# Feature-major operands turned by 32x32 block transposes on VectorE, and the first two column blocks of two projections multiplied by turns

## The chip, the cores and the metric

The kernel runs on one core of one Trainium2 chip. The metric is the time of one execution on the device in microseconds (us). Before the change the median of three runs is 1024.64 us (1023.89 to 1025.12).

## The reference

One layer of a decoder trunk, 256 tokens by 2048 features, everything in float32. A normalised input is multiplied by one wide matrix; three branches (block-sparse attention A, windowed attention B, a gated linear recurrence C) are built from its columns, each is gated and projected back to 2048 features, weighted by a sigmoid gate, and the three are summed. What the change touches comes after that:

```python
merged = jnp.einsum('bsnd,bsnd->bsd', gates, y_d)       # sum of the three gated branches
x = x + merged @ w_out                                  # 2048 x 2048
x = x + jax.nn.sigmoid(rmsnorm(x, ple_norm_g) @ w_pg) * (p_i @ w_pp)   # w_pg: 2048 x 2048
# output: rmsnorm(x, final_norm_g)
```

## The kernel before

**Tiling.** TensorE (PE) multiplies with the contracted features on the 128 partitions. An operand in "feature-major" form has features on partitions and the 256 tokens along the row; a result comes out "token-major", two halves (h = 0, 1) of 128 tokens on partitions and 512 columns of the output (one column block) along the row. A product over 2048 features takes 16 steps (k) of 128 features. Full precision is reached with three passes: both operands are split into a high part (a rounded copy, made by ScalarE, ACT) and a low part (the rest, made by VectorE, DVE), and `mm3` issues high x high, high x low, low x high. So a column block of `project` is 16 steps x 2 halves x 3 = 96 matmuls of 128x512.

**Weights.** They stream from memory in tiles of 128x1024, that is, two steps k of a column block; `fetch` loads one on SP's queue, `split` casts it on ACT (L112, `wh`) and subtracts on DVE (L113, `wl`). There are four buffers for raw tiles (`wraw`) and four for split ones (`wsp`): tile number i+4 can be cast only after PE has done with tile i.

**The two stages around the change.** `merge` (L618) runs for the three branches; for the last of them (`bi == 2`), after each of the four column blocks n, DVE multiplies the branch by its gate (L631), adds it into `merged` (L632), and `turn` (L604) brings these 512 features of `merged` to feature-major form, as operand `m` (`mT`) of the product with `w_out`. That loop (L654) computes column block after column block; for each, DVE adds the residual (L657, which also frees the PSUM tile), ACT sums squares (L660), and `turn` makes the operand `x2` of the product with `w_pg`, multiplied by the norm's gain (`split_scaled`, L191). The last loop (L678) multiplies by `w_pg`, applies the sigmoid and writes the output.

**`turn` before.** For 512 features it issues 8 transposes of 128x128 on PE (L610, a matmul against an identity) into two PSUM tiles `tp`, four into each. Then the halves are split from PSUM: without a gain an ACT copy (L180) and a DVE subtract (L181) of 128x512 for each of the two tiles; with a gain four ACT scalings (L193) and four DVE operations (L194) of 128x256. It is called eight times, four times for `m`, four times for `x2`.

**PSUM.** Products write to one of two tiles (`matrix_psum`, two banks for each), `tp` comes from four other banks.

**Order of the work.** Each engine runs its queue in order. A planner writes the queues at build time: among the instructions that are ready in its own timing model it takes the one that stands first in the program, except that a weight tile's cast and subtract are moved up by `LEAD` = 100 places (`high_priority`, L106). A tile of a column block takes 13 places in the program, its load and its 12 matmuls. DVE's queue holds, besides the `wl` subtractions, everything named DVE above.

Of the kernel before, what the change touches and what calls it, by code (L numbers as in the profile page):

```python
# [17 lines left out]
P = 128  # L18
D = 2048
SEQ = 256  # L20
NH = SEQ // P
BW = D // 2
KD = D // P
KB = BW // P
CW = 512
WT = 1024
# [11 lines left out]
NEG = -1e30  # L38
SLOT = 2112
WPAD = 64  # L40
WOFF = 32
RV = 384
B_ORDER = [g0 * 4 + s * 4 + i for g0 in (0, 2) for i in range(4) for s in range(2)]
# [3 lines left out]
def trunk(ctx: ExitStack, tc: tile.TileContext, x, xt, p, table, onehot, maskv, w_in, sinks, conv, w_ri, vec, fin, w_br,  # L47
          w_out, w_pg, w_pgt, w_pp, out):
    nc = tc.nc
# [9 lines left out]
    def block(name, dtype=F32):  # L59
        return blk.tile([P, SLOT], dtype, tag="blk", name=name)  # L60
# [4 lines left out]
    def cols(k, n=1):  # L65
        return slice(k * SEQ, (k + n) * SEQ)

    def aux(name):
        return ps_x.tile([P, CW], F32, tag="aux", name=name)

    def temp(name):
        return small.tile([P, 4, SEQ], F32, tag="tmp", name=name, bufs=4)

    ident = const.tile([P, P], F32, name="ident")
# [18 lines left out]
    def fetch(src, i, name, pieces=1):  # L93
        r = wraw.tile([P, WT], F32, tag="raw", name=f"r_{name}")
        n = WT // pieces
        for j in range(pieces):
            loads.append(nc.sync.dma_start(r[:, j * n : (j + 1) * n], src[i][:, j * n : (j + 1) * n]).ins)
        raws[name] = r, pieces

    def split(name, off):  # L100
        r, pieces = raws.pop(name)
        hi = wsp.tile([P, WT + WPAD], F32R, tag="whi", name=f"wh_{name}")[:, off : off + WT]
        lo = wsp.tile([P, WT + WPAD], F32R, tag="wlo", name=f"wl_{name}")[:, off : off + WT]
        n = WT // pieces
# [11 lines left out]
    def mm3(ps, a, b, first, last):  # L116
        (ah, al), (bh, bl) = a, b
        nc.tensor.matmul(ps, ah, bh, start=first, stop=False)  # L118
        nc.tensor.matmul(ps, ah, bl, start=False, stop=False)  # L119
        nc.tensor.matmul(ps, al, bh, start=False, stop=last)  # L120

    def weights_of(src, row, name, sub, off=0):
        held = {}

        def get(k):
            s = k // sub
            if s not in held:
                key = f"{name}_{s}"
                if key not in raws:
                    fetch(src, row + s, key)  # L130
                held[s] = split(key, off)
            return held[s], k % sub

        return get

    def matrix_psum(name):
        return ps_mm.tile([P, NH, CW], F32, tag="mm", name=f"ps_{name}")

    def project(act, src, row, name, cw=CW, weights=None, half=None, hooks={}):
        nk = len(act)  # L140
        if half is None:
            ps = matrix_psum(name).rearrange("p h c -> p (h c)")
        else:
            ps = aux(f"ps_{name}_{half}")
        get = weights or weights_of(src, row, name, WT // cw)
        for k in range(nk):
            w, kk = get(k)
            if k in hooks:
                with tc.issue_after(casts[-1]):
                    hooks[k]()  # L150
            c = slice(kk * cw, (kk + 1) * cw)
            for h in range(NH) if half is None else [half]:
                o = h * cw if half is None else 0
                q = slice(h * P, (h + 1) * P)
                mm3(ps[:, o : o + cw], [t[:, q] for t in act[k]], [t[:, c] for t in w],
                    k == 0 and o % CW == 0, k == nk - 1 and (half is not None or (o + cw) % CW == 0))
        return ps if half is not None else ps[:, : NH * cw].rearrange("p (h c) -> p h c", h=NH)

    def project_turned(row, name):
        ps = matrix_psum(name)  # L160
        get = weights_of(w_in, row, name, WT // SEQ, WOFF)
        for k in range(KD):
# [11 lines left out]
    def act_of(*units):  # L174
        return [tuple(t[:, cols(k)] for t in u) for u in units for k in range(KB)]

    def split_act(u, k, n, src):
        uh, ul = u
        o = cols(k, n)
        ins = nc.scalar.copy(uh[:, o], src).ins  # L180
        nc.vector.tensor_tensor(ul[:, o], src, uh[:, o].bitcast(F32), op=ALU.subtract)  # L181
        return ins
# [8 lines left out]
    def split_scaled(pair, src, scale):  # L191
        hi, lo = pair
        ins = nc.scalar.activation(hi, src, AF.Copy, scale=scale).ins  # L193
        nc.vector.scalar_tensor_tensor(lo, src, scale, hi.bitcast(F32), op0=ALU.mult, op1=ALU.subtract)  # L194
        return ins
# [70 lines left out]
    for b in range(4):  # L266
        t = block(f"h{b}", F32R)
# [28 lines left out]
    for n in range(4):  # L296
        ps = project(act_of(pT)[:2], w_pp, n, f"pp{n}")
        o = token_major(temp(f"pp{n}"))
# [303 lines left out]
    mT = []  # L602

    def turn(u, n, src, name, gain=None):  # L604
        for j in range(0, 4, 2):
            pt = aux(f"tp_{name}{n}{j}")
            for i in range(2):
                for h in range(NH):
                    c = n % 2 * CW + (j + i) * P
                    nc.tensor.transpose(pt[:, i * SEQ + h * P : i * SEQ + (h + 1) * P], src[:, h, c : c + P], ident)  # L610
            k = n % 2 * 4 + j
            if gain is None:
                split_act(u, k, 2, pt)
            else:
                for i in range(2):
                    split_scaled([t[:, cols(k + i)] for t in u], pt[:, cols(i)], gain[:, 4 * n + j + i : 4 * n + j + i + 1])

    def merge(z, bi, br):  # L618
        if bi == 0:
# [32 lines left out]
    x2T = [unit("x20"), unit("x21")]  # L652
    sq2 = const.tile([P, NH, 4], F32, name="sq2")
    for n in range(4):  # L654
        ps = project(act_of(*mT), w_out, n * KD * CW // WT, f"out{n}")
        sl = xr[n // 2][:, :, half_cols(n)]
        nc.vector.tensor_tensor(sl, ps, sl, op=ALU.add)  # L657
        junk = token_major(temp(f"jy{n}"))
        for h in range(NH):
            nc.scalar.activation(junk[:, h, :], sl[:, h, :], AF.Square, accum_out=sq2[:, h, n : n + 1])  # L660
        turn(x2T[n // 2], n, xr[n // 2], "x2", ple_g)
# [16 lines left out]
    for n in range(5):  # L678
        cw = CW if n < 3 else HW
        at = n * CW if n < 3 else 3 * CW + (n - 3) * HW  # L680
        b, lc = at // BW, slice(at % BW, at % BW + cw)
        if n < 3:
            parts = project(act_of(*x2T), w_pg, n * KD * CW // WT, f"pg{n}")
        elif n == 3:
            parts = project(act_of(*x2T), w_pgt, 0, f"pg{n}", cw=HW)
        y = token_major(temp(f"y{n}"))
        junk = token_major(temp(f"jz{n}"))
        ws = weights_of(w_pgt, KD * HW // WT, f"pg{n}", WT // HW)
        for h in range(NH):
            if n == 4:  # L690
                ps = project(act_of(*x2T), None, 0, f"pg{n}", cw=HW, weights=ws, half=h)[:, :HW]
            else:
                ps = parts[:, h, :]
            yh, xh = y[:, h, :cw], xr[b][:, h, lc]
            nc.scalar.activation(yh, ps, AF.Sigmoid, scale=rs2[:, h : h + 1])
            nc.vector.tensor_tensor(yh, yh, pps[b][:, h, lc], op=ALU.mult)
            nc.vector.tensor_tensor(xh, xh, yh, op=ALU.add)
            if n < 4:
                nc.scalar.activation(junk[:, h, :cw], xh, AF.Square, accum_out=sq3[:, h, n : n + 1])
                nc.gpsimd.tensor_tensor(xh, xh, fg[:, at : at + cw], op=ALU.mult)  # L700
                continue
            t, r = tot3[:, h : h + 1], rs3[:, h : h + 1]
            nc.vector.tensor_tensor_reduce(junk[:, h, :cw], xh, xh, op0=ALU.mult, op1=ALU.add, scale=1.0,
                                           scalar=0.0, accum_out=t)
            nc.vector.tensor_scalar(t, t, 1.0 / D, part[:, h : h + 1], op0=ALU.mult, op1=ALU.add)
            nc.gpsimd.tensor_tensor(r, t, half_c[:, :1], op=ALU.pow)
            nc.vector.tensor_tensor(xh, xh, fg[:, at : at + cw], op=ALU.mult)
            for eng, c0, c1 in ((nc.sync, 0, BW), (nc.scalar, BW + CW, D), (nc.sync, BW, BW + CW)):
                sl = xr[c0 // BW][:, h, c0 % BW : c0 % BW + c1 - c0]
                if eng is nc.sync:  # L710
                    nc.vector.tensor_scalar_mul(sl, sl, r)
                else:
                    nc.scalar.activation(sl, sl, AF.Copy, scale=r)
                eng.dma_start(out[h * P : (h + 1) * P, c0:c1], sl)
        if n == 3:
            nc.vector.reduce_sum(part, sq3, axis=AX.X)
            nc.vector.tensor_scalar(part, part, 1.0 / D, EPS, op0=ALU.mult, op1=ALU.add)
# [80 lines left out]
```

## Time and profile before

| | before |
|---|---|
| median of three runs | 1024.64 us |
| profiled execution | 1025.27 us |
| its span, first to last instruction | 1023.5 us |
| PE busy | 1011.1 us (99% of the span), 5216 matmuls |
| DVE busy | 643.5 us (63%) |
| ACT busy | 540.9 us (53%) |
| mean granted TensorE clock | 0.997 of 2.4 GHz |

An engine's busy time is the time in which at least one of its instructions runs. Matmuls overlap one another (each is recorded with some 0.39 us, and the next begins 0.23 us later), so what a matmul costs is read from the distance of starts, not from its duration. PEld is the load of a matmul's stationary operand, which runs beside the matmuls. The profiled execution is 1.8 us longer than its span.

### The profile page before, as it was taken

To read this page: it belongs to the slowest core of one execution; us is meant where nothing else is said; L and a number is where in the kernel's file an instruction comes from. 1 tells how busy PE (TensorE), PEld (TensorE's weight loads), DVE (VectorE), ACT (ScalarE), POOL (GpSimd) and SP (SyncE) were. 2 spreads that over 40 slices of the span, in tenths; PEclk is the share of its full clock that TensorE was granted. 3 is DMA by queue.
4 is the path that set the end of the run, shared out by engine and by line. 5 is a ranking of instruction groups with operands and counts; after the bars stand their busy time and mean duration, and the time that the engine had idled before them with its cause. 6 is when DMAs were issued, how large, how long until landed. Compare 5 with 4: busy or idle time off the path is not lost.

```text
span 1023.5 us, 13704 instructions
## 1 busy us (share of the span) xinstructions
PE 1011.1 (99%) x5216; PEld 860.2 (84%) x5216; DVE 643.5 (63%) x923; ACT 540.9 (53%) x762; POOL 30.2 (3%) x22
## 2 busy tenths in 40 slices
PE   8999999999999999999999999999999999999996
PEld 7788888888888888888988888888888888888886
DVE  5866956668866755456556677667545555555564
ACT  6744445558567654444445656655444444444552
POOL 0000000000000000000000001000000000000122
PEclk9999999999999999999999999999999999999998
DMA  9866655554646555555554555465555665576552
GB/s 330 291 220 214 202 194 176 181 174 156 206 165 209 178 174 201 188 191 196 185 187 158 190 188 184 144 199 171 183 187 185 223 236 180 187 271 224 201 184 84
DMA packets 58201, 199.52 MB, mean 195 GB/s; under 512 B 6600, under 2 KB 10008, under 8 KB 57624
## 3 DMA queue, kind: packets, MB, share of 16 engines
q1 hardware_dynamic: 51840, 186.41, 54.8%
q10 hardware_dynamic: 6296, 12.24, 3.4%
q8 instruction: 41, 0.67, 0.3%
q14 instruction: 24, 0.20, 0.1%
HBM read 194.40 MB, written 4.23 MB: 194 GB/s over the span
## 4 chain that ended last, share of the span: by engine, by line
PE 96%; DMA 2%; issue 1%; ACT 0%; DVE 0%; SPq 0%; POOLq 0%; POOL 0%; ACTq 0%; DVEq 0%
PE ps_in L166 21%; PE ps_in L168 11%; PE ps_in L119 10%; PE ps_in L118 10%; PE ps_in L120 10%; PE ps_out L120 3%; PE ps_out L118 3%; PE ps_out L119 3%; PE ps_pg L118 3%; PE ps_pg L119 3%; PE ps_pg L120 3%; PE ps_bra L120 1%; PE ps_bra L119 1%; PE ps_bra L118 1%; PE ps_brc L119 1%; PE ps_brc L118 1%
## 5 line engine op out<-in xcount | busy, mean ns | idle before, releaser
L113 DVE TENSOR_TENSOR wl_in<-r_in,wh_in 128x1024 fp32r<-128x1024 f32 x232 | 288.7, 1251 | 183.3 <-ACT wh_in L112 181.3
L112 ACT CAST wh_in<-r_in 128x1024 fp32r<-128x1024 f32 x232 | 242.9, 1050 | 268.1 <-PE ps_in L166 142.8
L166 PE MATMUL ps_in<-h,wh_in 128*128 128x512 f32 x928 | 289.9, 393 | 0.0
L168 PEld LDWEIGHTS ps_in<-h,wl_in 128*128 128x128 f32 x928 | 173.6, 188 | 39.4
L119 PE MATMUL ps_in<-wl_in,h 128*128 128x512 f32 (+1 forms) x480 | 184.7, 385 | 0.7 <-DVE wl_in L113 0.7
L168 PE MATMUL ps_in<-h,wl_in 128*128 128x256 f32 x928 | 185.0, 280 | 0.0
L118 PE MATMUL ps_in<-wh_in,h 128*128 128x512 f32 (+1 forms) x480 | 184.4, 385 | 0.0
L120 PE MATMUL ps_in<-wh_in,h 128*128 128x512 f32 (+1 forms) x480 | 183.8, 383 | 0.0
L166 PEld LDWEIGHTS ps_in<-h,wh_in 128*128 128x128 f32 x928 | 142.3, 188 | 0.2
L119 PEld LDWEIGHTS ps_in<-wl_in,h 128*128 128x128 f32 x480 | 90.3, 188 | 18.7 <-DVE wl_in L113 1.1
L118 PEld LDWEIGHTS ps_in<-wh_in,h 128*128 128x128 f32 x480 | 90.3, 188 | 17.6
L120 PEld LDWEIGHTS ps_in<-wh_in,h 128*128 128x128 f32 x480 | 90.3, 188 | 17.2
L113 DVE TENSOR_TENSOR wl_pg<-r_pg,wh_pg 128x1024 fp32r<-128x1024 f32 x32 | 39.8, 1243 | 38.3 <-ACT wh_pg L112 38.3
L113 DVE TENSOR_TENSOR wl_out<-r_out,wh_out 128x1024 fp32r<-128x1024 f32 x32 | 39.2, 1224 | 37.4 <-ACT wh_out L112 37.4
L112 ACT CAST wh_out<-r_out 128x1024 fp32r<-128x1024 f32 x32 | 33.7, 1054 | 42.5 <-PE ps_out L120 36.5
L112 ACT CAST wh_pg<-r_pg 128x1024 fp32r<-128x1024 f32 x32 | 33.7, 1052 | 41.9 <-PE ps_pg L120 33.5
L120 PE MATMUL ps_pg<-wh_pg,x_lo 128*128 128x512 f32 (+1 forms) x160 | 55.4, 347 | 0.0
L119 PE MATMUL ps_pg<-wl_pg,x_hi 128*128 128x512 f32 (+1 forms) x160 | 55.3, 347 | 0.0
L118 PE MATMUL ps_pg<-wh_pg,x_hi 128*128 128x512 f32 (+1 forms) x160 | 55.3, 347 | 0.0
L119 PE MATMUL ps_out<-wl_out,m_hi 128*128 128x512 f32 x128 | 50.1, 391 | 0.0
L118 PE MATMUL ps_out<-wh_out,m_hi 128*128 128x512 f32 x128 | 49.9, 390 | 0.0
L120 PE MATMUL ps_out<-wh_out,m_lo 128*128 128x512 f32 x128 | 49.8, 389 | 0.0
(273 smaller groups left out, 1271.4 us busy)
## 6 DMA issues: line engine op xcount, KB each, us to landing
r_in<-w_in_dram SPq DMA_DIRECT2D x232, 512.0 KB, 3.5
r_out<-w_out_dram SPq DMA_DIRECT2D x32, 512.0 KB, 3.4
r_pg<-w_pg_dram SPq DMA_DIRECT2D x24, 512.0 KB, 3.5
r_brc<-w_br_dram SPq DMA_DIRECT2D x16, 512.0 KB, 3.5
r_bra<-w_br_dram SPq DMA_DIRECT2D x16, 512.0 KB, 3.8
r_brb<-w_br_dram SPq DMA_DIRECT2D x16, 512.0 KB, 4.0
r_pg<-w_pgt_dram SPq DMA_DIRECT2D x8, 512.0 KB, 4.2
x<-xt_dram SPq DMA_DIRECT2D x4, 512.0 KB, 7.2
```

The source lines that it names most:

```text
L112: casts.append(nc.scalar.copy(hi[:, c], r[:, c]).ins)
L113: nc.vector.tensor_tensor(lo[:, c], r[:, c], hi[:, c].bitcast(F32), op=ALU.subtract)
L118: nc.tensor.matmul(ps, ah, bh, start=first, stop=False)
L119: nc.tensor.matmul(ps, ah, bl, start=False, stop=False)
L120: nc.tensor.matmul(ps, al, bh, start=False, stop=last)
L166: nc.tensor.matmul(ps[:, j, :], wh[:, cs[j]], h_both[k], start=k == 0, stop=False)
L168: nc.tensor.matmul(ps[:, j, SEQ:], wl[:, cs[j]], h_act[k][0], start=False, stop=k == KD - 1)
```

## The change

`turn` no longer uses PE. It takes a temporary in SBUF and fills it with 16 VectorE transposes: each reads 32 partitions (one quarter of the tokens of a half, index q) and writes 32 partitions (one quarter of the features, index f), 256 elements in each row, as eight blocks of 32x32 (two halves x four groups of 128 features). The source quarter q changes with every instruction, the destination quarter f with every fourth. The splits then read this temporary: without a gain one ACT copy and one DVE subtract of 128x1024 in place of two of each of 128x512, with a gain four and four as before, from SBUF in place of PSUM.

The second part reorders matmuls. `project_two` allocates two PSUM tiles and multiplies column blocks 0 and 1 by turns: steps k = 0 to 11 of block 0, the same of block 1, then k = 12 to 15 of block 0, then of block 1. It is used for `w_out` and `w_pg`; blocks 2 and 3 are as before. What follows block 0 (residual, squares, `turn`; or sigmoid and output) and what follows block 1 now both come after `project_two` in the program.

```diff
+    def project_two(act, src, names, late):
+        pss = [matrix_psum(n) for n in names]
+        gets = [weights_of(src, i * KD * CW // WT, n, WT // CW) for i, n in enumerate(names)]
+        for ks in (range(late), range(late, KD)):
+            for ps, get in zip(pss, gets):
+                for k in ks:
+                    w, kk = get(k)
+                    c = slice(kk * CW, (kk + 1) * CW)
+                    for h in range(NH):
+                        q = slice(h * P, (h + 1) * P)
+                        mm3(ps[:, h], [t[:, q] for t in act[k]], [t[:, c] for t in w], k == 0, k == KD - 1)
+        return pss
...
     def turn(u, n, src, name, gain=None):
-        for j in range(0, 4, 2):
-            pt = aux(f"tp_{name}{n}{j}")
-            for i in range(2):
-                for h in range(NH):
-                    c = n % 2 * CW + (j + i) * P
-                    nc.tensor.transpose(pt[:, i * SEQ + h * P : i * SEQ + (h + 1) * P], src[:, h, c : c + P], ident)
-            k = n % 2 * 4 + j
-            if gain is None:
-                split_act(u, k, 2, pt)
-            else:
-                for i in range(2):
-                    split_scaled([t[:, cols(k + i)] for t in u], pt[:, cols(i)], gain[:, 4 * n + j + i : 4 * n + j + i + 1])
+        t = temp(f"tn_{name}{n}")
+        c0 = n % 2 * CW
+        quad = [slice(i * QD, (i + 1) * QD) for i in range(P // QD)]
+        for f in quad:
+            for q in quad:
+                d = t[f].rearrange("p j (h q) -> p h j q", h=NH)[:, :, :, q]
+                s = src[q, :, c0 : c0 + CW].rearrange("p h (j f) -> p h j f", j=4)[:, :, :, f]
+                nc.vector.transpose(d, s)
+        k = n % 2 * 4
+        if gain is None:
+            split_act(u, k, 4, t.rearrange("p j q -> p (j q)"))
+        else:
+            for i in range(4):
+                split_scaled([o[:, cols(k + i)] for o in u], t[:, i, :], gain[:, 4 * n + i : 4 * n + i + 1])
...
     for n in range(4):
-        ps = project(act_of(*mT), w_out, n * KD * CW // WT, f"out{n}")
+        if n == 0:
+            pss = project_two(act_of(*mT), w_out, ["out0", "out1"], KD - 4)
+        ps = pss[n] if n < 2 else project(act_of(*mT), w_out, n * KD * CW // WT, f"out{n}")
...
-        if n < 3:
+        if n == 0:
+            two = project_two(act_of(*x2T), w_pg, ["pg0", "pg1"], KD - 4)
+        if n < 2:
+            parts = two[n]
+        elif n == 2:
             parts = project(act_of(*x2T), w_pg, n * KD * CW // WT, f"pg{n}")
```

## Rows read from the trace of the kernel before

**Rows 1.** The page: span, busy time of each engine (share), and its chain.

```profile
span 1023.5 us, 13704 instructions
PE 1011.1 (99%) x5216; PEld 860.2 (84%) x5216; DVE 643.5 (63%) x923; ACT 540.9 (53%) x762; POOL 30.2 (3%) x22
PE 96%; DMA 2%; issue 1%; ACT 0%; DVE 0%; SPq 0%; POOLq 0%; POOL 0%; ACTq 0%; DVEq 0%
```

**Rows 2.** All waits of PE: waiter, whom for, us in total, times, longest.

```profile
PE ps_pp L118 <- ACT wh_pp L112: 1.4, 1, 1.4
PE busy L262 <- DVE sp L353: 1.1, 1, 1.1
PE ps_in L119 <- DVE wl_in L113: 0.7, 1, 0.7
PE ps_pp L119 <- DVE wl_pp L113: 0.2, 1, 0.2
```

**Rows 3.** Tiles tp: instructions, count, duration min/median/max in ns, first and last start.

```profile
L610 PE MATMUL tp_m<-ident,merged x32: 270/272/273, 742.2 to 843.6; 128*128 128x128 f32 x32
L181 DVE TENSOR_TENSOR m_lo<-tp_m,m_hi x8: 681/682/683, 744.7 to 845.9; 128x512 fp32r<-128x512 f32 x8
L610 PE MATMUL tp_x<-ident,xr x32: 270/272/273, 863.0 to 932.0; 128*128 128x128 f32 x32
L194 DVE SCALAR_TENSOR_TENSOR x_lo<-tp_x,vecs,x_hi x16: 474/478/484, 865.2 to 934.6; 128x256 fp32r<-128x256 f32 x16
```

**Rows 4.** PE's timeline around one turn: start us, us, instruction.

```profile
842.39 0.39 PE L119 MATMUL ps_out<-wl_out,m_hi 128*128 128x512 f32 x1
842.61 0.39 PE L120 MATMUL ps_out<-wh_out,m_lo 128*128 128x512 f32 x1
842.85 1.03 PE L610 MATMUL tp_m<-ident,merged 128*128 128x128 f32 x8
843.64 0.48 PE L118 MATMUL ps_out<-wh_out,m_hi 128*128 128x512 f32 x1
843.95 0.40 PE L119 MATMUL ps_out<-wl_out,m_hi 128*128 128x512 f32 x1
844.18 0.39 PE L120 MATMUL ps_out<-wh_out,m_lo 128*128 128x512 f32 x1
```

**Rows 5.** The chain of waits, four of its eight steps at a turn: start, us.

```profile
742.41 0.87 PE tp_m L610 x8
775.94 0.87 PE tp_m L610 x8
...
863.17 0.87 PE tp_x L610 x8
885.82 0.87 PE tp_x L610 x8
```

**Rows 6.** DVE's groups by shape: count, busy us, mean ns, idle before.

```profile
L113 DVE TENSOR_TENSOR wl_out<-r_out,wh_out 128x1024 fp32r<-128x1024 f32 x32 | 39.2, 1224 | 37.4 <-ACT wh_out L112 37.4
L476 DVE TENSOR_SCALAR e_b<-e_b,st1b 128x256 f32<-128x256 f32 x16 | 5.6, 351 | 0.3
L657 DVE TENSOR_TENSOR xr<-ps_out,xr 128x1024 f32<-128x1024 f32 x4 | 4.9, 1223 | 1.2 <-PE ps_out L120 1.2
L632 DVE TENSOR_TENSOR merged<-merged,sg_b 128x1024 f32<-128x1024 f32 x4 | 4.9, 1219 | 0.0
L450 DVE TENSOR_TENSOR_SCAN xcT<-rg,ig 128x256 f32<-128x256 f32 x8 | 4.9, 677 | 0.0
L181 DVE TENSOR_TENSOR zb_lo<-gb,zb_hi 128x256 fp32r<-128x256 f32 x8 | 3.4, 421 | 0.5 <-ACT zb_hi L180 0.5
```

**Rows 7.** DVE's timeline: a pair on changing partitions, then a pair on all partitions.

```profile
570.05 0.86 DVE L559 TENSOR_TENSOR gb<-py_b,gb 64x256 f32<-64x256 f32 x2 [0.99 <-PE py_b L488]
570.94 0.42 DVE L460 CUSTOM_DVE_ANT_0 e_b<-s_b,bias_b 128x256 f32<-128x256 f32 x1
...
865.24 0.87 DVE L194 SCALAR_TENSOR_TENSOR x_lo<-tp_x,vecs,x_hi 128x256 fp32r<-128x256 f32 x2
```

**Rows 8.** Timelines of PE's last matmul of out0, then DVE and ACT.

```profile
856.43 0.39 PE L120 MATMUL ps_out<-wh_out,m_lo 128*128 128x512 f32 x1
...
857.53 1.23 DVE L657 TENSOR_TENSOR xr<-ps_out,xr 128x1024 f32<-128x1024 f32 x1 [0.41 <-PE ps_out L120]
...
863.02 1.05 ACT L112 CAST wh_out<-r_out 128x1024 fp32r<-128x1024 f32 x1 [1.67 <-PE ps_out L120]
...
864.10 1.23 DVE L113 TENSOR_TENSOR wl_out<-r_out,wh_out 128x1024 fp32r<-128x1024 f32 x1 [1.49 <-ACT wh_out L112]
```

**Rows 9.** ACT's timeline: a cast that waited for its load.

```profile
924.00 1.05 ACT L112 CAST wh_pg<-r_pg 128x1024 fp32r<-128x1024 f32 x1 [2.70 <-DMA r_pg<-w_pg_dram]
```

More of the change, by code (lines that the diff above doesn't have):

```diff
@@ L40 @@
 WPAD = 64
+QD = 32
 WOFF = 32
```

## The prediction

> **What bounds the kernel now.** I read the page first: PE is busy for 99% of the span and holds 96% of the chain that ended last [rows 1]. Then all waits of PE: there are four, 3.4 us together, on tiles of the opening (the side projection `pp`, a warm-up, the first weight of `in`), none on a tile of the stages that change [rows 2]. So TensorE never waits in the two stages that change, and time is won or lost there in two ways only: matmul work that goes away, and waits that appear. Third, the timeline of PE around one turn, for what the removed transposes cost; fourth, DVE's groups and timeline, since DVE takes the work over.
>
> **The PE work removed.** A transpose is recorded with 272 ns [rows 3], but PE's instructions overlap, so this is not its price. In the timeline the matmul at 842.61 us is followed by 8 transposes and then by three matmuls, the third at 844.18, 1.57 us later [rows 4]. Without transposes three matmuls take 0.68 us: a 128x512 matmul every 0.2267 us (842.39 to 842.61 shows one step, rounded). So a turn costs 1.57 - 0.68 = 0.89 us. The chain gives it a second time: 775.94 - 742.41 = 33.53 us is 144 matmuls of a merge step (32.64) and 0.89; 885.82 - 863.17 = 22.65 us is 96 matmuls (21.76) and 0.89 [rows 5]. There are eight turns, all on the path: 8 x 0.89 = **7.1 us removed**.
>
> **The DVE work added.** Eight times 16 transposes of 32 partitions x 256 elements. The trace of before has no such instruction. The nearest rows with 256 elements in a row: one with a single source and a scalar takes 351 ns, a two-source one 421 ns, a scan 677 ns [rows 6]. Spacing matters as much as duration. Two operations on all partitions overlap: a pair of 478 ns [rows 3] takes 0.87 us, so the second begins 0.39 us after the first, 0.09 early. The pair that writes partitions 0 to 63 and then 64 to 127 does not: 0.86 us for two of 0.42, and the operation after it, back on all partitions, begins at 570.94, again with no overlap [rows 7]. The transposes change their source partitions every time, so I take the spacing of this last pair: T = **0.44 us** (0.86 - 0.42). The bounds: 0.27 us (351 ns with 0.08 of overlap) and 0.69 us (677 ns and no overlap). I stay at 0.44 because a transpose reads and writes every element once, without a scalar or a sum, which is nearest to the 421 ns row. The price is never below nothing: DVE gives no time back to a PE that does not wait.
>
> The Trainium skill, page VectorE: DVE Perf Modes, section Two Vector instructions with no wait between them, has a rule for this: an instruction whose input or output begins in another group of 32 partitions than the last one's starts only when all earlier ones have finished. The pair in [rows 7] agrees. By the rule 16 transposes take 7.0 us; by the overlap of the other pair they would take 16 x 0.35 = 5.6 us, and the sum below would then have almost no stall (that is the first rival).
>
> So a turn holds DVE for 16 x 0.44 = 7.0 us. The splits after it cost the same as before (1.22 us for one 128x1024 in place of two of 0.68 that overlap, or four of 0.44).
>
> **Where DVE's lateness reaches PE.** A weight tile feeds 12 matmuls, 2.72 us. DVE must subtract one every 2.72 us, 1.23 us each; it has 1.49 us to spare in each period [rows 6, 8]. A cast waits for PE to free the buffer four tiles back [rows 8], so a subtraction is ready about 2.5 us into the three tiles (8.2 us) that lie before its use, and 5.7 us of lateness cost nothing.
>
> *Merge steps 0 to 2*: 12 subtractions (14.8 us), two operations of 1.23, the transposes 7.0 and the split 1.2 make 25.5 us of DVE in 32.6 us of PE. Nothing waits for the result yet. Cost 0.
>
> *Last turn of `m`*: its operand is needed at k = 12. Block 0 alone would give 12 x 6 x 0.2267 = 16.3 us; with block 1 put between it is 32.6 us, against the same 25.5 us at most, all subtractions done first. Cost 0; it is hidden by the first 144 matmuls of `project_two`.
>
> *Turns 0 and 1 of `x2`*: these become late, because blocks 0 and 1 of `out` now end 5.44 us (24 matmuls) apart, not 21.76. Count from the last matmul of block 0. Block 1 takes 5.44 us, then block 2 uses its tile j at 5.44 + 2.72 j, the subtracted part 0.23 later: tile 7 is needed at 24.7 us. Now DVE's queue by the planner's rule. With block 2's first place as 0, turn 0 holds the places -54 to -28, turn 1 -27 to -1 (1 residual, 2 squares, 16 transposes, 8 splits each), and tile j's subtraction -99 + 13 j. So tiles 1 to 6 come before or within the turns, but tile 7, at -8, stands behind all 32 transposes, which are ready by then. DVE has to do before tile 7 is finished: the start 0.87 us after the last matmul (857.53 against 856.43 + 0.23 [rows 8]), two residuals 2.46, seven subtractions 8.61, 32 x 0.44 = 14.08, and the first turn's four splits 1.75; in sum 27.8 us. PE waits 27.8 - 24.7 = **3.1 us** in the last quarter of block 2. The next tile has its own 2.7 us more and arrives in time, within some tenths.
>
> *Turns 2 and 3*: each has a column block of its own. Ahead of tile 7 stand one residual, five open subtractions and 16 transposes, 15 us, against 19 us. For turn 3, needed 32.6 us after `out3`, the whole stretch from the end of block 0 (81.6 us of PE) holds 30 subtractions 36.9, four residuals and splits 11.9 and 64 T = 28.2, together 77 us; it fits as long as T is below 0.5. Cost 0, with 4 us of cover.
>
> *PSUM*: `out2` needs block 0's tile, freed by its residual 2.1 us after block 0, with 5.4 us of room. `pg2` needs the two sigmoids of `pg0`, also with 5.4. *Loads*: the same bytes in nearly the same order; before, a cast came 2.70 us late because of a load and PE did not wait [rows 2, 9]. Cost 0, at worst about that 2.7 us where it meets DVE's lateness.
>
> **Sum.** The profiled execution took 1025.27 us (span 1023.5 and 1.8 around it), 0.63 more than the median of the runs. 1025.27 - 7.1 + 3.1 = 1021.2; less 0.63 that is **1020.5 us** for the median (rounded).
>
> **The rivals.** *No stall.* The transposes overlap or are shorter (T at most 0.34), or the planner's queue has tile 7's subtraction ahead of some transposes of turn 1. For it: the 351 ns row; against it: the pair on changing partitions. Then only the removed work counts: 1024.64 - 7.1 = 1017.5 us.
>
> *DVE becomes the bound (the other side).* The place is the stretch from `out0`'s end to the last quarter of `pg0`. If a float32 transpose takes as long for an element as the scan, T = 0.69: tile 7 is ready at 13.7 + 22.1 = 35.8 us, and PE waits 11.1 us; the whole-stretch count (48.8 + 44.2 = 93 against 81.6) gives 11.4. Time 1017.5 + 11.4 = 1029 us. The loss equals the gain at 13.7 + 32 T - 24.7 = 7.1, T = 0.565. For it: only the scan's row; a scan has a feedback from element to element, a transpose none.
>
> *The last turn is late in spite of `project_two`.* If the planner puts ACT's `x_hi` or `m_hi` far behind casts, PE waits at k = 12. The room is 6.7 us for `m` and 4 us for `x2`, so a loss of 1 to 3 us beside the forecast: 1022 to 1024 us.
>
> **How the numbers follow.** Forecast (T 0.36 to 0.50, stall 0.5 to 5 us): 0.47, its own range 1018 to 1022.3. No stall: 0.32. DVE bound or near it (T above 0.5): 0.16, of which 0.06 within 2 us of before. Last turn late: 0.05, slightly faster than before or the same. A difference of 0.2% (2 us) is what a measurement of this kernel tells from none. Faster 0.82, same 0.07, slower 0.11. Range: 1016.9 (no stall, and the runs' scatter of 0.6) to 1024.3 (T = 0.55, stall 6.6).
>
> **What would show it.** Right: no L610 on PE in the two stages, 64 matmuls fewer; 128 transposes on DVE with starts 0.42 to 0.46 us apart; one wait of PE on `wl_out`, some 3 us, late in `out2`, and none at k = 12 of `out0` or `pg0`; DVE's busy time up by about 56 us. Wrong: no wait of PE at all (then 1017.5), starts 0.5 us or more apart, a wait on `m` or `x2`, or a residual that keeps `out2` waiting for PSUM.

## The result, and the profile after

The median went from 1024.39 us (1023.89 to 1025.12, the three runs above and a fourth) to 1030.15 us (1028.63 to 1031.44, four runs): ratio 1.0054, 95% interval 1.0039 to 1.0069. The kernel became slower by 5.8 us (0.5%) where 4 us less were forecast, and the time lies above the forecast's range. The profiled execution took 1028.63 us, the fastest of the four; the others were 1.3 to 2.8 us longer, and their traces are not there to say where. All counts below are against this one execution, 3.4 us above that of before.

The page after: span, busy time of each engine with its share, and the shares of the chain of waits.

```profile
span 1026.8 us, 13690 instructions
PE 1006.9 (98%) x5152; PEld 855.2 (83%) x5152; DVE 698.4 (68%) x1047; ACT 539.8 (53%) x758; POOL 29.7 (3%) x22
PE 90%; DVE 5%; DMA 2%; issue 1%; ACT 1%; SPq 0%; POOLq 0%; ACTq 0%; POOL 0%; DVEq 0%
```

Against [rows 1]: the 64 transposes are gone from PE, DVE has 54.9 us more work (forecast: about 56), and 5% of the chain now lies on DVE. All waits of PE after (waiter, whom for, us in total, times, longest):

```profile
PE ps_pg L120 <- DVE wl_pg L114: 5.5, 1, 5.5
PE ps_out L120 <- DVE wl_out L114: 3.3, 2, 2.2
PE ps_pp L119 <- ACT wh_pp L113: 1.2, 2, 0.9
PE busy L276 <- DVE sp L367: 1.1, 1, 1.1
```

The last two belong to the opening, as all did before [rows 2]. The first two rows are three new waits for subtractions of weights. In PE's timeline after (start us, us, instruction, in brackets the idle time ahead of it and what ended it) they stand here:

```profile
888.32 0.39 PE L119 MATMUL ps_out<-wh_out,m_hi 128*128 128x512 f32 x1
890.92 0.51 PE L120 MATMUL ps_out<-wl_out,m_hi 128*128 128x512 f32 x1 [2.21 <-DVE wl_out L114]
891.26 0.40 PE L121 MATMUL ps_out<-wh_out,m_lo 128*128 128x512 f32 x1
...
909.90 0.39 PE L119 MATMUL ps_out<-wh_out,m_hi 128*128 128x512 f32 x1
911.33 0.50 PE L120 MATMUL ps_out<-wl_out,m_hi 128*128 128x512 f32 x1 [1.04 <-DVE wl_out L114]
...
927.56 0.39 PE L119 MATMUL ps_pg<-wh_pg,x_hi 128*128 128x512 f32 x1
933.46 0.80 PE L120 MATMUL ps_pg<-wl_pg,x_hi 128*128 128x512 f32 x1 [5.51 <-DVE wl_pg L114]
934.05 0.63 PE L121 MATMUL ps_pg<-wh_pg,x_lo 128*128 128x512 f32 x1
934.48 0.63 PE L119 MATMUL ps_pg<-wh_pg,x_hi 128*128 128x512 f32 x1
```

Distances of starts, less the 0.23 us of a normal step, give the loss. In `out2`: 2.60 - 0.23 = 2.37, and 0.11 at the next step, together 2.5 us. In `out3`: 1.20 + 0.11 = 1.3 us. In `pg0`: 5.67 + 0.36, and then matmuls 0.43 us apart instead of 0.23 up to 937 us. The windows show the reason for the last part (stretch, length, busy time of PE, PEld, DVE, ACT, POOL, granted clock of PE, busy share of the DMA engines, GB/s):

```profile
891.00:896.00 5.00, 5.00 (x22) 4.12 (x23) 4.85 (x8) 0.00 (x0) 0.00 (x0) 1.00 0.67 206
933.50:937.00 3.50, 3.50 (x8) 2.78 (x9) 3.50 (x5) 0.32 (x1) 1.16 (x1) 0.51 0.74 188
```

The granted clock was 0.51 after the gap in `pg0`, the 1.2 GHz level: eight matmuls in 3.5 us where 1.8 would do, 1.7 us, of which 0.36 is counted already. So `pg0` lost 5.67 + 0.36 + 1.35 = 7.4 us. All three: 2.5 + 1.3 + 7.4 = 11.2 us. With 7.1 saved that is 4.1 more; the waits of the opening are 1.1 less than in [rows 2], which leaves 3.0 of the 3.3 us by which the span grew.

**How the loss in `pg0` came about.** DVE's timeline, then ACT's, of the same stretch after:

```profile
916.78 1.22 DVE L114 TENSOR_TENSOR wl_pg<-r_pg,wh_pg 128x1024 fp32r<-128x1024 f32 x1
922.50 1.23 DVE L114 TENSOR_TENSOR wl_pg<-r_pg,wh_pg 128x1024 fp32r<-128x1024 f32 x1 [4.51 <-ACT wh_pg L113]
923.65 1.22 DVE L675 TENSOR_TENSOR xr<-ps_out,xr 128x1024 f32<-128x1024 f32 x1
924.90 7.18 DVE L626 STREAM_TRANSPOSE tn_x<-xr 32x256 f32<-32x256 f32 x16
932.19 3.49 DVE L114 TENSOR_TENSOR wl_pg<-r_pg,wh_pg 128x1024 fp32r<-128x1024 f32 x3
```

```profile
911.92 0.33 ACTq L687 DMA_DIRECT2D pp<-pp_d  x1
912.77 0.45 ACTq L690 DMA_DIRECT2D fg<-fin_dram  x1
921.42 1.05 ACT L113 CAST wh_pg<-r_pg 128x1024 fp32r<-128x1024 f32 x1 [5.40 <-DMA r_pg<-w_pg_dram]
924.90 0.63 ACT L678 ACTIVATE jy<-xr 128x512 f32<-128x512 f32 x1 [2.43 <-DVE xr L675]
926.16 2.25 ACT L113 CAST wh_pg<-r_pg 128x1024 fp32r<-128x1024 f32 x2
```

Read it as two things that meet: a late cast, and an order. ACT issues 3 MB of loads for the tail (`pp`, `fg`) at 912 us; while they run, the cast of the second `w_pg` tile waits 5.40 us for its own load (the first was subtracted at 916.78). DVE idles 4.51 us for that cast, subtracts at 922.50, and only then comes to the last residual, which stands behind it in its queue. That makes the residual late by 1.1 us, not by more: the last matmul of `out3` starts at 922.12 us, and a residual that nothing holds up starts 0.43 us after it (after `out0`: 869.03 and 869.46), so 922.55 where 923.65 was measured.

The larger part is the order of DVE's queue, which is fixed when the program is built. Only two subtractions of `w_pg` stand ahead of the residual; behind the residual come the 16 transposes of the last turn, 7.18 us in one piece, and behind them the third tile's subtraction (932.19), which PE needs at 927.8. ACT had that tile's cast ready before (926.16; it stands behind the squares, which wait 2.43 us for the residual). An estimate from these rows: with the cast on time and the same queues, PE would still have waited 5.67 - 1.1 = 4.6 us. Before the change the same load collision made a cast 2.70 us late [rows 9] and PE did not notice.

### The profile page after: what moved, and what is told of

Same layout as the page of the kernel before. It is cut to its first block, busy times and chain, and to the rows that moved or that the text cites. A ratio compares the mean times of both kernels' runs of the same rounds, so it can differ in the third digit from the quotient of the medians.

```text
span 1026.8 us, 13690 instructions
## 1 busy us (share of the span) xinstructions
PE 1006.9 (98%) x5152; PEld 855.2 (83%) x5152; DVE 698.4 (68%) x1047; ACT 539.8 (53%) x758; POOL 29.7 (3%) x22
## 4 chain that ended last, share of the span: by engine, by line
PE 90%; DVE 5%; DMA 2%; issue 1%; ACT 1%; SPq 0%; POOLq 0%; ACTq 0%; POOL 0%; DVEq 0%
PE ps_in L180 21%; PE ps_in L182 11%; PE ps_in L120 10%; PE ps_in L119 10%; PE ps_in L121 10%; PE ps_pg L120 3%; PE ps_pg L121 3%; PE ps_pg L119 3%; DVE tn_x L626 2%; PE ps_bra L121 1%; PE ps_bra L120 1%; PE ps_bra L119 1%; PE ps_brc L120 1%; PE ps_brc L119 1%; PE ps_brc L121 1%; PE ps_brb L121 1%
```

## The experiments

Theories: **Q**, blocks of 16 transposes stand ahead of subtractions in DVE's queue, and that alone makes PE wait; **R**, multiplying the two column blocks by turns is at fault; **L**, the loads of `pp` and `fg` are at fault; later **Q+L**, in `pg0` it takes both. Every median stands beside the kernel before on the same chip (1024.69 to 1024.72). `turn_pe` is `turn` as it was.

**Only `m` is turned on DVE.**

```diff
-        turn(x2T[n // 2], n, xr[n // 2], "x2", ple_g)
+        turn_pe(x2T[n // 2], n, xr[n // 2], "x2", ple_g)
```

> The changed kernel, but the four turns of x2 go back to PE transposes; the four turns of m stay on VectorE and both products still multiply their first two blocks by turns. Theory Q (the queue: VectorE's queue holds blocks of 16 transposes of x2 in front of weight subtractions that PE needs): no wait of PE on wl_out or wl_pg is left, only four turns of 0.89 us are saved, 1024.4 - 3.6 = 1020.8 us. Theory R (the multiplying by turns itself is at fault, since what follows blocks 0 and 1 comes in one heap): waits in out2 and pg0 stay, 1025 us or more. Theory L (the 3 MB of loads of pp and fg that arrive at out3's end hold up the weights of pg0): the wait in pg0 stays, some 7 us, and the time is about 1028 us.

Measured 1020.79 us, ratio 0.9961 (0.9947 to 0.9976). PE waits only in the opening, 1.4 us in two places. Four turns should save 3.6 us, and 3.9 were saved. All of the loss comes with the turns of `x2`.

**Both turns on PE, the column blocks still by turns.** The body of `turn` is the old one, everything else as after.

```diff
-        t = temp(f"tn_{name}{n}")
+        for j in range(0, 4, 2):
+            pt = aux(f"tp_{name}{n}{j}")
...
```

> The second part of the change alone: all eight turns by PE transposes, the first two blocks of both products multiplied by turns. Theory Q: as before, 1024.4 us within 1 us, no wait of PE after the opening. Theory R: slower than before by several us. Theory L: as before, since the loads were there before and PE did not wait for them.

Measured 1024.69 us, ratio 1.000 (0.9991 to 1.001), no wait of PE after the opening. `project_two` by itself costs nothing and gains nothing; R in its simple form, without the DVE turns, is out.

**The column blocks one after the other, turns on DVE.**

```diff
-        if n == 0:
-            pss = project_two(act_of(*mT), w_out, ["out0", "out1"], KD - 4)
-        ps = pss[n] if n < 2 else project(act_of(*mT), w_out, n * KD * CW // WT, f"out{n}")
+        ps = project(act_of(*mT), w_out, n * KD * CW // WT, f"out{n}")
...
-        if n == 0:
-            two = project_two(act_of(*x2T), w_pg, ["pg0", "pg1"], KD - 4)
-        if n < 2:
-            parts = two[n]
-        elif n == 2:
+        if n < 3:
```

> The first part of the change alone: all turns on VectorE, no multiplying by turns. In the changed kernel the operand m was complete 16 us after out0 had begun, and block 0 alone gives 16.3 us until k = 12, so PE waits 0 to 1 us there. Theory Q: turns of x2 come 21.8 us apart again, so nothing bunches in out2 and out3, but each turn is still 16 transposes in one piece: the waits in out2 and out3 go (together 3.9 us), the one at pg0 stays at 5 to 7 us or grows by what k = 12 needs: 1024.4 - 7.1 + 6 to 10 = 1023 to 1027 us. Theory R: 1017.5 to 1019 us, since the reordering was the fault. Theory L: 1024 us, the wait in pg0 alone is left.

Measured 1026.86 us, ratio 1.0022 (1.0012 to 1.0031). Of the three waits only that in `pg0` is left:

```profile
PE ps_pg L120 <- DVE wl_pg L114: 5.7, 1, 5.7
PE ps_pg L119 <- ACT wh_pg L113: 0.4, 1, 0.4
```

This lies in Q's range. By the distances of starts PE loses 9.3 us there, about 2.3 of it at the lower clock; 1024.7 - 7.1 + 9.3 = 1026.9. Three things follow. The waits in `out2` and `out3` come from the order by turns together with the DVE turns; the prediction had counted that for `out2`, not for `out3`. The wait in `pg0` does not need `project_two`. And at k = 12 of `out0`, with one column block's time for the last turn of `m` instead of two, PE did not wait: the cover that `project_two` gives was not needed there.

**The loads of `pp` and `fg` issued earlier**, behind the eighth cast of `project_two` on `w_out`; the rest as after.

```diff
+            c0 = len(casts)
             pss = project_two(act_of(*mT), w_out, ["out0", "out1"], KD - 4)
+            pps = [wide(block(f"pp{h}")) for h in range(2)]
+            fg = block("fg")
+            with tc.issue_after(casts[c0 + 7]):
+                for h in range(2):
+                    nc.scalar.dma_start(pps[h], pp_d[h])
+                nc.scalar.dma_start(fg[:, :D], ...)
```

> The changed kernel with one thing moved: the loads of pp and fg (3 MB) are queued on ScalarE early in out1 in place of out3's end; all other queues stay as they were. Theory L: the wait of 5.9 us in pg0 is gone, with it the slow matmuls after it, 1030.2 - 7.4 = 1022.8 us. Theory Q: the 16 transposes of turn 3 still stand in front of the subtractions of pg0; the cast that came 5.4 us late comes on time, so the wait shrinks to 1 to 3 us, with the waits in out2 and out3 unchanged (2.5 and 1.4 us): 1025 to 1027 us.

Measured 1021.99 us, ratio 0.9973 (0.9963 to 0.9982): 8.2 us less than after, for three transfers in another place, and nearer to L's time than to Q's. The wait in `pg0` is gone although turn 3 still stands on DVE; a cast of `w_out` now waits 7.27 us for its load, where no transposes stand behind it, and PE loses 0.2 us. One of PE's waits, ACT's cast, and a window of this kernel (columns as above):

```profile
PE ps_out L120 <- DVE wl_out L114: 2.2, 1, 2.2
```

```profile
854.06 1.06 ACT L113 CAST wh_out<-r_out 128x1024 fp32r<-128x1024 f32 x1 [7.27 <-DMA r_out<-w_out_dram]
```

```profile
892.00:895.30 3.30, 3.30 (x9) 2.61 (x8) 3.18 (x7) 0.00 (x0) 0.00 (x0) 0.50 0.63 196
```

But the expectation that all other queues stay as they were did not hold. Three subtractions of `w_pg` (917.48, 919.65 and 921.61 us) now stand ahead of DVE's last residual, and a fourth ahead of the transposes:

```profile
923.47 1.23 DVE L682 TENSOR_TENSOR xr<-ps_out,xr 128x1024 f32<-128x1024 f32 x1 [0.63 <-PE ps_out L121]
924.61 1.22 DVE L114 TENSOR_TENSOR wl_pg<-r_pg,wh_pg 128x1024 fp32r<-128x1024 f32 x1
925.74 7.17 DVE L626 STREAM_TRANSPOSE tn_x<-xr 32x256 f32<-32x256 f32 x16
```

The changed kernel had two. So with the place of the loads the planner wrote another order, and this run changes two things at once: when the weight tiles arrive, and how many subtractions go ahead of the block.

The wait in `out2` stays as it was after, and is followed by 3.3 us at half clock, 1.7 us more; `out3` waits no longer. Sum: 1024.7 - 7.1 + 2.5 + 1.7 = 1021.8.

**Turn 3 of `x2` alone back on PE**, loads in place: the other half of Q+L.

```diff
-        turn(x2T[n // 2], n, xr[n // 2], "x2", ple_g)
+        (turn_pe if n == 3 else turn)(x2T[n // 2], n, xr[n // 2], "x2", ple_g)
```

> The changed kernel, the loads of pp and fg where they were, but turn 3 of x2 goes back to PE; the other seven turns stay on VectorE. Theory Q+L (the wait in pg0 needs both: loads that delay weight tiles, and 16 transposes that stand between the late subtractions): the wait in pg0 and the slow matmuls after it go, those of out2 and out3 stay (3.8 us): 1030.2 - 7.4 + 0.9 = 1023.7 us. Theory L alone (the loads suffice): the wait stays at 4 us or more, 1028 us or more.

Measured 1022.23 us, ratio 0.9972 (0.9962 to 0.9982), some 1.5 us below what was expected. The expectation started from the median after, and the profiled run in which the waits were read is 1.5 us faster; from the kernel before, seven turns and two waits give 1024.7 - 7 x 0.89 + 3.8 = 1022.3. The waits in `out2` and `out3` stand as after, that in `pg0` is gone; beside this row of PE's waits there are only three of the opening:

```profile
PE ps_out L120 <- DVE wl_out L114: 3.3, 2, 2.2
...
```

So with the loads in place and no transposes there is no wait in `pg0`, and with the transposes and the loads elsewhere there is none. It takes both, and Q+L held; but "the loads" means their place in the program, which acts through the late cast (1.1 us) and through the order of the queues (the rest). No run has the one without the other.

**`project_two` on `w_pg` alone.** The first half of the third experiment's diff.

> The changed kernel, but the product with w_out goes column block by column block again; w_pg keeps the multiplying by turns. Theory Q+L: out2 and out3 lose their waits (3.8 us), since the turns of x2 come one by one; no wait at k = 12 of out0, since none was there with the first part alone; the wait in pg0 stays, some 7 us with its slow matmuls: 1024.7 - 7.1 + 7.4 = 1025 us (1024 to 1026.5). A rival (out0 needs the cover): a wait of 1 us or more in out0.

Measured 1026.57 us, ratio 1.0021 (1.0012 to 1.003). After the opening PE waits in `pg0` only, 6 us and the lower clock behind it, as without any `project_two`. The median lies just above the expected range, since the loss there is 8.1 us by the distances of starts, not 7.4.

**The same, and the loads later**, behind the ninth cast of `w_pg`: the order by turns in `w_out` and the early place of the loads both taken away.

```diff
-        if n == 0:
-            pss = project_two(act_of(*mT), w_out, ["out0", "out1"], KD - 4)
-        ps = pss[n] if n < 2 else project(act_of(*mT), w_out, n * KD * CW // WT, f"out{n}")
+        ps = project(act_of(*mT), w_out, n * KD * CW // WT, f"out{n}")
...
+            c0 = len(casts)
             two = project_two(act_of(*x2T), w_pg, ["pg0", "pg1"], KD - 4)
+            with tc.issue_after(casts[c0 + 8]):
+                for h in range(2):
+                    nc.scalar.dma_start(pps[h], pp_d[h])
+                nc.scalar.dma_start(fg[:, :D], ...)
```

> As two_on_pg_only, and the loads of pp and fg are queued on ScalarE behind the ninth cast of w_pg, when turn 3 is over and before pg0's results are used. Theory Q+L: PE has no wait left in these stages; eight turns saved, 1024.7 - 7.1 = 1017.6 us (1017 to 1018.5). If the late subtractions come from VectorE's load alone: a wait of 2 us or more stays in pg0, 1019.5 us or more.

Measured 1018.00 us (1017.23 to 1018.37), ratio 0.9933 (0.992 to 0.9945): the fastest here, 6.7 us below before. Waits of PE, then DVE at the last turn:

```profile
PE busy L276 <- DVE sp L367: 1.1, 1, 1.1
PE ps_in L120 <- DVE wl_in L114: 0.4, 1, 0.4
PE ps_pp L119 <- ACT wh_pp L113: 0.3, 1, 0.3
```

```profile
913.31 1.22 DVE L114 TENSOR_TENSOR wl_pg<-r_pg,wh_pg 128x1024 fp32r<-128x1024 f32 x1
915.12 1.23 DVE L114 TENSOR_TENSOR wl_pg<-r_pg,wh_pg 128x1024 fp32r<-128x1024 f32 x1 [0.59 <-ACT wh_pg L113]
917.84 1.23 DVE L114 TENSOR_TENSOR wl_pg<-r_pg,wh_pg 128x1024 fp32r<-128x1024 f32 x1 [1.49 <-ACT wh_pg L113]
919.48 1.23 DVE L673 TENSOR_TENSOR xr<-ps_out,xr 128x1024 f32<-128x1024 f32 x1 [0.41 <-PE ps_out L121]
920.62 1.22 DVE L114 TENSOR_TENSOR wl_pg<-r_pg,wh_pg 128x1024 fp32r<-128x1024 f32 x1
921.75 7.17 DVE L626 STREAM_TRANSPOSE tn_x<-xr 32x256 f32<-32x256 f32 x16
...
929.03 2.35 DVE L114 TENSOR_TENSOR wl_pg<-r_pg,wh_pg 128x1024 fp32r<-128x1024 f32 x2
```

The 16 transposes still stand in one piece ahead of the next subtraction (929.03 us). But no cast holds DVE up by more than 1.49 us, and the queue has four subtractions of `w_pg` ahead of them, where the changed kernel had two. `pg0` begins at 919.28 us, 0.20 before the residual; PE comes to its fifth tile's subtracted part at 919.28 + 4 x 2.72 + 0.23 = 930.4, and that is ready at about 930.2. The block fits with next to nothing to spare, and the saving is then the 7.1 us of the removed work (1024.72 - 7.1 = 1017.6).

**The loads later, the rest as after.**

```diff
+            c0 = len(casts)
             two = project_two(act_of(*x2T), w_pg, ["pg0", "pg1"], KD - 4)
+            with tc.issue_after(casts[c0 + 8]):
...
```

> The changed kernel with only the loads of pp and fg moved, here to the same late place (behind the ninth cast of w_pg). As with the earlier place the wait in pg0 goes; the waits in out2 and out3 stay (2.5 and 1.3 us, more if the granted clock falls after them): 1021.4 us (1021 to 1023).

Measured 1021.45 us, ratio 0.9963 (0.995 to 0.9977). Only `out2` waits after the opening (2.2 us by its row), again with about 1.7 us of lower clock behind it. What `project_two` on `w_out` costs beside the DVE turns is the difference to the run before: 3.5 us.

**No `project_two` at all, the loads later.** The third experiment's diff, and the loads behind the eighth cast of `pg0`.

> All turns on VectorE, no multiplying by turns at all, and the loads of pp and fg behind the eighth cast of w_pg. It asks whether the second part of the change is of use. In the changed kernel with the loads moved, the operand of turn 3 was complete 15.6 us after out3's end; block 0 of pg alone gives 16.3 us until k = 12. If the second part is not needed: no wait of PE, 1017.6 to 1018.3 us, as with it on w_pg. If it is needed: a wait in pg0 at k = 12 of 1 to 3 us, 1019 to 1021 us.

Measured 1020.11 us, ratio 0.9952 (0.9938 to 0.9966), better than before, 2 us worse than the best. At k = 12 of `pg0`, where a cover was thought needed, PE does not wait. It loses 1.8 us at the fourth tile of `pg1` instead. So the time lies in the range given for "needed", but by another wait. The moved loads now delay casts of `pg1`; the fourth tile's cast stands behind them and behind the sigmoid and squares of `pg0`. That the loads are the cause is argued from the late cast. ACT's row, and PE's waits:

```profile
940.80 1.05 ACT L113 CAST wh_pg<-r_pg 128x1024 fp32r<-128x1024 f32 x1 [4.47 <-DMA r_pg<-w_pg_dram]
```

```profile
PE ps_pg L120 <- DVE wl_pg L114: 1.0, 1, 1.0
PE ps_pg L119 <- ACT wh_pg L113: 0.3, 1, 0.3
```

Whether `project_two` on `w_pg` is worth something with loads in a harmless place is not settled: this run changed the place of the loads as well.

## Why the prediction was wrong, by its steps

*The PE work removed: right.* With the waits gone, the best kernel is 6.7 us below before where 7.1 was counted, and four turns gave 3.9 where 3.6 was counted.

*The DVE work added: right.* The tiles of the transposes after (count, duration min/median/max in ns, first and last start):

```profile
L626 DVE STREAM_TRANSPOSE tn_m<-merged x64: 432/436/441, 737.1 to 843.1; 32x256 f32<-32x256 f32 x64
L626 DVE STREAM_TRANSPOSE tn_x<-xr x64: 425/436/441, 871.7 to 931.6; 32x256 f32<-32x256 f32 x64
```

A block of 16 takes 7.18 us, 0.449 each against the forecast's 0.44. The Trainium skill, page VectorE: DVE Perf Modes, section Two Vector instructions with no wait between them, is borne out: the source group changes with every transpose, and the spacing (0.449) is no shorter than the duration (0.436).

*Merge steps 0 to 2, and the last turn of `m`: right.* No wait in either. The prediction named `project_two` as what hides the last turn; without it there was no wait either, so that cover was not needed.

*Turns 0 and 1 of `x2`: the size right by luck, the tile wrong.* 3.1 us were forecast in `out2`, 2.5 came. But the count had all 32 transposes ahead of tile 7. Here is DVE's queue after, from turn 0 to the wait:

```profile
871.73 7.18 DVE L626 STREAM_TRANSPOSE tn_x<-xr 32x256 f32<-32x256 f32 x16
878.94 1.23 DVE L114 TENSOR_TENSOR wl_out<-r_out,wh_out 128x1024 fp32r<-128x1024 f32 x1
...
885.08 2.22 DVE L626 STREAM_TRANSPOSE tn_x<-xr 32x256 f32<-32x256 f32 x5
...
887.82 1.79 DVE L626 STREAM_TRANSPOSE tn_x<-xr 32x256 f32<-32x256 f32 x4
889.64 1.23 DVE L114 TENSOR_TENSOR wl_out<-r_out,wh_out 128x1024 fp32r<-128x1024 f32 x1
```

The subtraction that PE waited for (889.64) stands behind 26 transposes, and it is the sixth of `out2`: the last matmul of `out0` starts at 869.03 us, `out2` 24 matmuls of `out1` later (874.70), and the wait falls 60 matmuls on, so this is tile 5, not tile 7. One term was misread besides: the residual starts 0.20 us after `out0`'s end (869.26 and 869.46), where the prediction had 0.87. It had taken the matmul at 856.43 us for the last of `out0` [rows 8]; that was the one at 857.11, by three blocks of 21.76 us and three turns of 0.89 back from the last of `out3` (925.07). Its count would then have given 2.4 us.

*Turns 2 and 3: the step that failed.* It said "Cost 0, with 4 us of cover". For turn 3 this came from a sum over the whole stretch, which does not see the order; for turn 2 from the assumption that five open subtractions go ahead of the 16 transposes and only tile 7 behind them. Turn 2 cost 1.3 us in `out3`, turn 3 cost 7.4 in `pg0`. The planner's queue had the transposes in one piece ahead of an earlier tile each time: 15 of turn 2 ahead of the subtraction at 910.05 us (the fifth tile of `out3`), which PE needed at 910.13 and had at 911.3, and 16 of turn 3 ahead of the third tile of `w_pg`. The prediction took the planner's order from its rule of places; the rule chooses among what is ready in the planner's own model, and that model is not in the trace.

*Loads: the other half of the failure.* "Cost 0, at worst about that 2.7 us where it meets DVE's lateness" rested on a row in which nothing slow stood behind the late cast. After, the cast waited 5.40 us for its load and made the last residual 1.1 us late, ahead of 7.18 us of transposes. More than that, the queues are not independent of the loads: with them elsewhere and nothing else changed in the program, DVE's queue had four subtractions ahead of turn 3 instead of two. Together the two steps cost 7.4 us in `pg0`, 1.35 of it given away at the lower clock. The place of the loads alone, or the transposes alone, cost PE nothing there.

*The sums.* The room for `m` is 32.6 - 25.5 = 7.1 us, not 6.7, and the forecast adds up to 1020.6, not 1020.5; neither matters to the outcome.

*The rivals.* "DVE becomes the bound" gave 1029 us, near the measured time, but its condition (T above 0.565) did not hold, and DVE idled 4.51 us just ahead of the long wait: it was late through the order of its queue, not through the amount of work. "No stall" is what the best experiment reached: 1018.0 against 1017.5. "The last turn is late" did not happen: PE waits for weights in all three places, never for `m` or `x2`.

**Open.** Why the planner put two subtractions ahead of turn 3 in one kernel and four in the other is not in a trace, and no run kept the order and changed the arrival of the weights alone; the 1.1 us and 4.6 us are read from rows, not measured by a run. The transposes were not spread by hand among the subtractions, which could take the waits away with `project_two` and the loads left as they are. That `out3` stops waiting in the two kernels with moved loads because the slow matmuls in `out2` gave DVE time is argued, not shown. And the 1.3 to 2.8 us by which the other executions of the changed kernel exceed the profiled one are not placed; their mean granted clocks are 0.992, 0.992 and 0.994, that of the profiled one 0.994.

## What to carry to other kernels

When work moves from a full engine to one with idle time, don't compare sums over a stretch: find the longest piece that an in-order queue will hold ahead of an instruction that the full engine waits for, and add to it whatever can make that piece start late. Read the order from the queue as it was built: here moving three loads changed how many subtractions stood ahead of the piece, and the same 7.1 us of saved work was worth +5.8 us or -6.7 us, by the place of three loads and the order of one loop. An order by turns that gives one operand more time takes it from the next one (`out2`), so read first whether the first operand was late at all.

## What the runs showed of the hardware that was not expected

A gap of PE can cost more than its length, and not always. After a gap of 2.6 us in `out2` the changed kernel ran on at full granted clock (1.00 in 891 to 896 us), while the kernel with earlier loads, with the same gap at the same place, was granted 0.50 (the 1.2 GHz level) for 3.3 us; the gap of 5.9 us in `pg0` was followed by 0.51 for 3.5 us. These two stretches cost 1.7 us each, of which 0.36 in `pg0` is the first step. The kernel with turn 3 on PE had the same gap in `out2` and no slow matmul after it, the one with later loads had it and was slowed again.

While three transfers of 1 MB on ACT's queue run, casts wait for 0.5 MB weight tiles on SP's: the longest such wait was 5.40 us after, 7.27 with the loads earlier and 4.47 in the last run; before the change it was 2.70 [rows 9]. In the changed kernel's windows, the DMA engines were busy throughout and moved over 350 GB/s:

```profile
912.00:918.00 6.00, 6.00 (x28) 4.97 (x27) 6.00 (x8) 3.50 (x6) 0.00 (x0) 1.00 0.93 358
918.00:924.00 6.00, 6.00 (x28) 4.95 (x28) 1.50 (x2) 1.05 (x1) 0.00 (x0) 1.00 1.01 422
```
